# SwiGLU blocks behind the mixers all as seven-product quads, in a streaming-encoder trunk

## The chip, the core and the metric

The kernel runs on one core of a Trainium2 chip. The time is what the device measures from start to end of one execution, in microseconds (us); smaller is better. The engines are PE (matmul, with PEld for its weight loads), DVE (vector), ACT (scalar), POOL and SP, which here only issues loads. Each works through its own queue of instructions in a fixed order, and semaphores hold an instruction until what it needs is there.

## What is computed

Two layers of an encoder trunk, 512 frames of width 1024, inner width 2816, all in float32. The part that matters here is the end of the mixer and the second SwiGLU of a layer:

```python
def rmsnorm(x, g):
    return x * rsqrt(mean(x * x, -1) + EPS) * g

def swiglu(x, w_gu, w_down):
    g, u = split(x @ w_gu, 2, axis=-1)
    return (silu(g) * u) @ w_down

for i in range(DEPTH):                       # DEPTH = 2
    h = h + 0.5 * swiglu(rmsnorm(h, ffn1_norm[i]), ffn1_w_gu[i], ffn1_w_down[i])
    ...
    h = h + merged @ w_o[i]
    h = h + 0.5 * swiglu(rmsnorm(h, ffn2_norm[i]), ffn2_w_gu[i], ffn2_w_down[i])
    ...
```

## The kernel before

**Layout and precision.** Activations stand transposed, as eight tiles h[k] of 128 channels by 512 tokens. Each float32 operand is split into a rounded part (hi) and the rest (lo), and a product takes three matmuls, hi x hi, hi x lo, lo x hi (`mm3`, L266). Weights come in chunks of 1024 columns: SP loads a raw chunk into one of ten buffers (`st`, L52), ACT casts hi (`wh`, L71) and DVE subtracts for lo (`wl`, L72), into four pairs of buffers.

**Whole blocks and quads.** The inner width is 22 blocks of 128. A *whole* block takes 48 matmuls of 512 columns, gate and up. A *quad* (class `Sevens`) makes two blocks, both with gate and up, by seven products on halves (Strassen in Winograd's form, two halves of the tokens, of the inputs and of the block pair). Products 1, 2, 6, 3, 4 are *joint* steps (`joint`, L520): 8 matmuls of 512 columns (wide) and 8 of 256 (narrow). Products 5 and 7 are 24 matmuls of 256 columns (`product`, L540). Four raw quarters a11, a21, a22, a12 of the weights are combined by DVE (class `Quad`, L130), and the sums of the tokens stand in `Halved`: `own` (L464) makes what needs one row of h, `other` (L476) what needs the row four further on, each with casts on ACT and subtractions on DVE. Sums in PSUM: product 1 goes to b, ACT copies b into a (`seed`, L549) where product 2 is added, product 6 goes on in b, ACT copies b into d, where 5 and 3 are added, and 7 and 4 go on in b.

**PSUM** has eight banks. `paired` (L223) gives them out as two pairs for b, one pair for a and d, and two single banks `mp` for downs, output products and 1/rms.

**The mixer's end.** Eight output products of 24 matmuls (L1058), each into a single bank, are added to h[m] by DVE (L1060). `normed` (L357) follows behind each: x[k] = h[k] times the gain, split on ACT and DVE, the square on ACT, the sum of squares on DVE.

**The second SwiGLU** (`ffn`, from L588; its names begin with b0 in layer 0 and b1 in layer 1). Two blocks are whole, 20 are in quads 1 to 10. PE computes block 0 (L712), then two matmuls for the mean of the squares (`rms`, L342), and ACT and DVE make 1/rms while PE does quad 1's product 1; block 1 stands between quad 1's steps. A finished pair of values is multiplied by 1/rms, goes through Silu and is split (`finish`, L599). The downs (`down`, L637) of four blocks into one output row are 12 matmuls on a bank into which ACT has written 2h and which ACT writes back halved; `fill` (L651) puts them between the steps of the following quads (`next_quad`, L656).

What sets the order: a scheduler places instructions on each engine's queue from the program's order and its own estimates; `issue_after` holds a group behind a named instruction.

Of the kernel before, what the change touches and what calls it, by code (L numbers as in the profile page):

```python
# [129 lines left out]
class Quad:  # L130


    def __init__(self, W, quarters):
        self.W = W
        for q in ("a11", "a21", "a22", "a12"):
            setattr(self, q, W.raw(quarters[q]))

    def part(self, j):

        W = self.W  # L140
        tt = W.nc.vector.tensor_tensor
        if j == 1:
# [16 lines left out]
        return W.split(self.a11)  # L159


# [21 lines left out]
def trunk_kernel(ctx, tc, dims, x, p, positions, gains, rope_c, final_row, weights, out):  # L183
# [19 lines left out]
    class Banks:  # L203
# [18 lines left out]

        def paired(self):  # L223
            self.close()
            self.chain, self.seeded, self.single = self.pool("bp", 2), self.pool("ap", 1), self.pool("mp", 2)

# [12 lines left out]
    def PA(name):  # L239
        return two(banks.seeded, name)  # L240

    def halves(t):
# [15 lines left out]
    def split_to(hi, lo, src, scale=None):  # L258
        if scale is None:
            nc.scalar.copy(hi, src)  # L260
            return nc.vector.tensor_tensor(lo, src, hi.bitcast(F32), ALU.subtract)
        else:
            nc.scalar.activation(hi, src, AF.Copy, scale=scale)  # L263
            return nc.vector.scalar_tensor_tensor(lo, src, scale, hi.bitcast(F32), ALU.mult, ALU.subtract)
# [91 lines left out]

    def normed(nm, l, name, after=None, paired=True):  # L357

        xs, sq = [], Squares(name)
        for k in range(KD):  # L360
            xs.append(split(h[k], f"{name}x{k}", gain(nm, l, k), paired))
            sq.add(h[k])
            if after:
                after(k, xs)
        return xs, sq.parts()
# [81 lines left out]
    class Halved:  # L447
# [11 lines left out]
        def row(self, j, xs):  # L459

            self.own(j, xs)
            self.other(j, xs)

# [12 lines left out]
        def other(self, j, xs):  # L476

            H = S // 2
            left, right = slice(0, H), slice(H, S)
            k = j + KD // 2  # L480
            x, t, th, tl = self.half.pop(j)
            y, u = G(f"{self.name}y{j}"), G(f"{self.name}u{j}")
            nc.scalar.mul(y, h[k], gain(self.nm, self.l, k))
            nc.vector.tensor_tensor(t[:, right], y[:, right], x[:, right], ALU.subtract)
            nc.vector.tensor_tensor(u[:, left], t[:, right], x[:, left], ALU.add)
            nc.vector.tensor_tensor(u[:, right], y[:, left], u[:, left], ALU.subtract)
            split_to(th, tl, t)
            self.ys[7].append((th[:, right], tl[:, right]))
            for p_, at in ((2, left), (3, right)):
                self.ys[p_].append(self.both(xs[k], at))  # L490
            for p_, at in ((6, left), (4, right)):
                v = G(f"{self.name}u{j}_{p_}", F32R).rearrange("p (a t) -> p a t", t=H)
                split_to(v[:, 0, :], v[:, 1, :], u[:, at])
                self.ys[p_].append((v[:, 0, :], v))

    class Sevens:
# [7 lines left out]
        def __init__(self, w, l, name, ys, columns, done):  # L504
            self.w, self.l, self.name, self.ys, self.columns, self.done = w, l, name, ys, columns, done
            self.todo = {}
            self.narrow_first = ()

# [10 lines left out]

        def joint(self, ps, d, j):  # L520

            hi, lo = d["w"].part(j)
            at = [slice(i * P, (i + 1) * P) for i in range(8)]
            def wide(last):
                for k, (_, pair) in enumerate(self.ys[j]):
                    for w in range(2):
                        nc.tensor.matmul(ps[:, w, :].rearrange("p (a t) -> p a t", t=self.H), hi[:, at[2 * k + w]], pair,
                                         start=j == 1 and k == 0, stop=last and k == 3, skip_group_check=True)

            def narrow(last):  # L530
                for k, (vh, _) in enumerate(self.ys[j]):
                    for w in range(2):
                        nc.tensor.matmul(ps[:, w, :self.H], lo[:, at[2 * k + w]], vh, start=False, stop=last and k == 3,
                                         skip_group_check=True)

            parts = (narrow, wide) if j in self.narrow_first else (wide, narrow)
            for i, part in enumerate(parts):
                part(i == 1)

# [9 lines left out]
        def seed(self, n, what):  # L549
            d = self.todo[n]  # L550
            d[what] = PA(f"{self.name}{n}{what}")
            nc.scalar.copy(d[what].rearrange("p w t -> p (w t)"), d["b"].rearrange("p w t -> p (w t)"))

        def out(self, n, ps, f, c):
            t = self.tile(n, f"o{f}{c}")
            nc.scalar.copy(t, ps[:, :, self.H:])
            nc.vector.tensor_tensor(t, ps[:, :, :self.H], t, ALU.add)
            self.done(n, f, c, t, t)

        def step(self, n, j):  # L560
# [26 lines left out]

    def ffn(l, nm, name, first=False, beside=iter(()), early=2):  # L588

# [4 lines left out]
        ys = Halved(nm, l, name)  # L594
        n_whole = 4 if first else 2
        n0 = n_whole // 2
# [18 lines left out]
        if not first:  # L615
            sevens.narrow_first = (3, 4, 6)

        def early_rows(k, xs):

            if 0 <= k - KD // 2 < early:  # L620
                ys.row(k - KD // 2, xs)

        xs, acc = normed(nm, l, name, early_rows)

# [26 lines left out]
        def fill():  # L651
            if downs:
                m, f0 = downs.pop(0)
                down(m, f0, f0 + 4)

        def next_quad(n):  # L656

            for i, j in enumerate((1, 4, None, 2, 6, None, 5, 7, 3, None, None)):
                next(beside, None)
                if j is None:  # L660
                    if i < 9 or downs and downs[0][1] < f_last:
                        fill()
                    continue
                step(n if j == 4 else n + 1, j)
                if j == 6 and n % 2:
                    downs.extend((m, 2 * n - 2) for m in range(KD))

# [9 lines left out]
        if first:  # L677
# [22 lines left out]
            activate(3)  # L700
            downs.extend((m, 0) for m in range(KD))
            fill()
# [5 lines left out]
            for _ in range(2):  # L708
                fill()
        else:  # L710
            pss[0] = whole(0)
# [14 lines left out]
        fill()  # L726
        for n in range(n0, np_ - 1):
            next_quad(n)

        f0 = f_last  # L730
        left = [m for m in range(KD) if (m, f0) in downs]
        assert len(left) == len(downs)
# [25 lines left out]
    def mixer(l):  # L758
# [292 lines left out]
        for m in range(KD):  # L1051
# [4 lines left out]
            merged.append(split(t, f"{name}mg{m}"))  # L1056
        banks.paired()
        for m in range(KD):  # L1058
            ps = proj(W.col("w_o", l, m * P, D), merged, f"{name}wop{m}")
            nc.vector.tensor_tensor(h[m], ps, h[m], ALU.add)  # L1060
# [196 lines left out]
    for l in range(DEPTH):  # L1257
        ffn(l, "ffn1", f"a{l}", l == 0, rotary() if l == 0 else iter(()), 2 if l else 0)
        mixer(l)
        ffn(l, "ffn2", f"b{l}")  # L1260
        (ple_last if l == DEPTH - 1 else ple)(l)
# [48 lines left out]
```

## Time and profile before

| what | value |
|---|---|
| time, median of 3 runs | 2252.38 us (2252.13 to 2253.1) |
| the profiled execution's own time | 2252.33 us |
| its span, first to last instruction | 2250.3 us |
| PEld, busy | 1947.7 us (87%) |
| DVE, busy | 1743.5 us (77%) |
| ACT, busy | 1456.1 us (65%) |
| HBM | 98 GB/s over the span |

The profile shows each instruction with its start, its duration and what ended the idle time before it. Matmuls are pipelined: a matmul of 512 columns shows a duration of 0.39 us, but the next starts 0.23 us behind it, so PE is measured here from start to start. On ACT and DVE too a row starts some 0.1 us before the shown end of the row ahead, if it waits for nothing.

### The profile page before, as it was taken

How to read it: one execution, taken by the hardware profiler on the slowest of the kernel's cores; microseconds unless marked ns; L12 is line 12 of the kernel's file. 1: busy time of each engine (PE TensorE's matmuls, PEld its weight loads, DVE VectorE, ACT ScalarE, POOL GpSimd, SP SyncE). 2: the span in 40 equal slices, each digit the busy share in tenths (PEclk: the TensorE clock that was granted, in tenths of full speed). 3: DMA queues.
4: the chain of work that ended last, by engine and by line, in shares of the span. 5: the costliest groups of instructions: out<-in, count | busy, mean ns of one | idle time of the engine just before them, and what ended most of it. 6: DMA issues, size and time to landing. Idle time of an engine off the chain costs nothing.

```text
span 2250.3 us, 31142 instructions
## 1 busy us (share of the span) xinstructions
PE 2240.8 (100%) x12144; PEld 1947.7 (87%) x12144; DVE 1743.5 (77%) x2453; ACT 1456.1 (65%) x2246; POOL 37.4 (2%) x42
## 2 busy tenths in 40 slices
PE   9999999999999999999999999999999999999998
PEld 8888888888888888888888888888888888888887
DVE  8987768788866887776798777687889678777756
ACT  7666666576744666667676666764767357666664
POOL 0000000000200000000000000000001000000000
PEclk9999999999999999999999999999999999999999
DMA  5333332323132232334223233323222223333321
GB/s 215 99 113 104 103 122 75 112 76 104 47 104 84 94 103 97 107 107 141 75 94 104 96 106 108 113 88 102 92 76 75 94 75 103 104 104 103 108 99 38
DMA packets 63362, 223.04 MB, mean 99 GB/s; under 512 B 7280, under 2 KB 7280, under 8 KB 63216
## 3 DMA queue, kind: packets, MB, share of 16 engines
q1 hardware_dynamic: 62640, 220.28, 29.2%
q8 instruction: 95, 1.56, 0.3%
q10 hardware_dynamic: 576, 0.79, 0.1%
q14 instruction: 51, 0.42, 0.1%
HBM read 218.94 MB, written 2.10 MB: 98 GB/s over the span
## 4 chain that ended last, share of the span: by engine, by line
PE 97%; DVE 2%; ACT 1%; issue 0%; DVEq 0%
PE a0pd L268 2%; PE a1pd L268 2%; PE b0pd L268 2%; PE b1pd L268 2%; PE a0pd L269 2%; PE a0pd L270 2%; PE b1pd L269 2%; PE b0pd L269 2%; PE a1pd L269 2%; PE b1pd L270 2%; PE b0pd L270 2%; PE a1pd L270 2%; PE m0mop L268 1%; PE m1mop L269 1%; PE m0mop L269 1%; PE m1mop L270 1%
## 5 line engine op out<-in xcount | busy, mean ns | idle before, releaser
L72 DVE TENSOR_TENSOR wl<-st,wh 128x1024 fp32r<-128x1024 f32 (+1 forms) x508 | 614.7, 1212 | 227.5 <-ACT wh L71 224.1
L71 ACT CAST wh<-st 128x1024 fp32r<-128x1024 f32 (+1 forms) x507 | 527.9, 1044 | 306.6 <-PE m1Bp L269 13.9
L71 ACT CAST wh<-s 128x1024 fp32r<-128x1024 f32 x49 | 51.6, 1052 | 28.8 <-PE m1Cp L269 4.2
L72 DVE TENSOR_TENSOR wl<-s,wh 128x1024 fp32r<-128x1024 f32 x49 | 59.6, 1216 | 0.3 <-ACT wh L71 0.3
L152 DVE TENSOR_TENSOR st<-st,st 128x1024 f32<-128x1024 f32 x49 | 59.7, 1219 | 0.2
L154 DVE TENSOR_TENSOR s<-st,st 128x1024 f32<-128x1024 f32 x49 | 59.6, 1217 | 0.1
L149 DVE TENSOR_TENSOR st<-st,s 128x1024 f32<-128x1024 f32 x49 | 59.6, 1216 | 0.0
L157 DVE TENSOR_TENSOR st<-st,st 128x1024 f32<-128x1024 f32 x49 | 59.6, 1216 | 0.0
L644 ACT ACTIVATE h<-a0pd 128x512 f32<-128x512 f32 x40 | 23.7, 594 | 5.6 <-PE a0pd L270 5.3
L644 ACT ACTIVATE h<-b1pd 128x512 f32<-128x512 f32 x40 | 23.7, 592 | 4.9 <-PE b1pd L270 4.8
L644 ACT ACTIVATE h<-b0pd 128x512 f32<-128x512 f32 x40 | 23.7, 592 | 4.7 <-PE b0pd L270 4.6
L644 ACT ACTIVATE h<-a1pd 128x512 f32<-128x512 f32 x40 | 23.6, 591 | 4.5 <-PE a1pd L270 4.4
L640 ACT ACTIVATE a1pd<-h 128x512 f32<-128x512 f32 x40 | 24.0, 599 | 0.7
L640 ACT ACTIVATE b1pd<-h 128x512 f32<-128x512 f32 x40 | 23.9, 599 | 0.6
L640 ACT ACTIVATE b0pd<-h 128x512 f32<-128x512 f32 x40 | 23.9, 598 | 0.6
L640 ACT ACTIVATE a0pd<-h 128x512 f32<-128x512 f32 x40 | 23.9, 598 | 0.6
L107 POOL MEMSET wh<- 128x256 f32 x4 | 1.1, 314 | 1173.3 <-DVE wl L72 1173.3
L268 PE MATMUL a0p<-a0x,wh 128*128 128x512 f32 x44 | 17.1, 390 | 0.0
L269 PE MATMUL a0p<-a0x,wh 128*128 128x512 f32 x44 | 17.1, 390 | 0.0
L270 PE MATMUL a0p<-a0x,wl 128*128 128x512 f32 x44 | 17.1, 389 | 0.0
L263 ACT ACTIVATE b0x<-h,cols 128x512 fp32r<-128x512 f32 x8 | 5.8, 724 | 13.3 <-DVE h L1060 13.3
L263 ACT ACTIVATE b1x<-h,cols 128x512 fp32r<-128x512 f32 x8 | 5.8, 723 | 13.3 <-DVE h L1060 13.3
(6945 smaller groups left out, 7503.9 us busy)
## 6 DMA issues: line engine op xcount, KB each, us to landing
st<-in_weights SPq DMA_DIRECT2D x406, 512.0 KB, 3.3
h<-in_x SPq DMA_DIRECT2D x8, 256.0 KB, 5.4
st<-in_weights SPq DMA_DIRECT2D x7, 256.0 KB, 5.3
out<-e1d SPq DMA_DIRECT2D x4, 256.0 KB, 2.1
out<-fh SPq DMA_DIRECT2D x3, 256.0 KB, 2.2
e0pi<-in_p SPq DMA_DIRECT2D x2, 256.0 KB, 3.5
e1pi<-in_p SPq DMA_DIRECT2D x2, 256.0 KB, 3.8
fg<-in_final_row SPq DMA_DIRECT2D x2, 256.0 KB, 4.5
```

The lines of the kernel that those rows point to most:

```text
L71: self.nc.scalar.copy(hi[:, w], src[:, w])
L72: self.nc.vector.tensor_tensor(lo[:, w], src[:, w], hi[:, w].bitcast(F32), ALU.subtract)
L149: tt(self.a12, self.a12, self.s, ALU.subtract)
L152: tt(self.a11, self.a11, self.a21, ALU.subtract)
L154: tt(self.s, self.a22, self.a11, ALU.subtract)
L157: tt(self.a21, self.a21, self.a22, ALU.add)
L263: nc.scalar.activation(hi, src, AF.Copy, scale=scale)
L268: nc.tensor.matmul(ps, wh, vh, start=first, stop=False, skip_group_check=seeded)
L269: nc.tensor.matmul(ps, wh, vl, start=False, stop=False, skip_group_check=seeded)
L270: return nc.tensor.matmul(ps, wl, vh, start=False, stop=last, skip_group_check=seeded)
L640: nc.scalar.mul(ps, h[m], 2.0)
L644: nc.scalar.mul(h[m], ps, 0.5)
```

## The change

In the second SwiGLU of both layers (`quads=True`) blocks 0 and 1 become quad 0, and there are no whole blocks.

- The weights of quad 0 are loaded and combined while the mixer's output product runs (`early`): parts 1 and 2 are split in halves of 512 columns into activation buffers, the sums for the other five are made at once.
- The output products are done in the order 0, 4, 1, 5, 2, 6, 3, 7, two of them into one tile of two banks, in turn the pair of a and d and a third pair (`PX`). `normed` follows the same order, and behind each row come `own` or `other`, so the last row of token sums stands ahead of the cast of the squares and of 1/rms.
- PE then does quad 0's product 1, the wide half of quad 1's product 1, the two matmuls for 1/rms (into the third pair), quad 0's 2 and 6, the narrow half of quad 1's product 1, quad 0's 5, 7, 3 (d of quad 0 in the third pair). Then the third pair is given back as two single banks.
- Blocks 0 and 1 go down alone (6 matmuls for each output row), then 2 and 3; the rest in fours as before.

The core of the diff:

```diff
+    def early(self, split):
+        tt = self.W.nc.vector.tensor_tensor
+        self.ready[1] = split(self.a11)
+        self.ready[2] = split(self.a12)
+        tt(self.a11, self.a11, self.a21, ALU.subtract)
+        self.s = self.W.buffer("s")
+        tt(self.s, self.a22, self.a11, ALU.subtract)
+        tt(self.a12, self.a12, self.s, ALU.subtract)
+        tt(self.a21, self.a21, self.a22, ALU.add)
+        self.summed = True
...
-        def paired(self):
+        def paired(self, spare=False):
...
+            if spare:
+                whole, self.scope = self.scope, ExitStack()
+                self.spare = self.pool("xp", 1)
+                self.part, self.scope = self.scope, whole
+            else:
+                self.single = self.pool("mp", 2)
+        def spare_to_singles(self):
+            self.part.close()
+            self.single = self.pool("mp", 2)
...
+            j = k - KD // 2
+            if quads:
+                ends[:] = [ys.own(k, xs) if j < 0 else ys.other(j, xs), split_to.hi]
...
+                if n == 0 and j == 1 and quads:
+                    sevens.seed(1, "a")
+                else:
+                    step(n if j == 4 else n + 1, j)
+                if j == 6 and (n % 2 or quads and n == 0):
+                    downs.extend((m, max(2 * n - 2, 2 if quads and n else 0), 2 * n + 2) for m in range(KD))
...
+        elif quads:
+            sevens.where[0, "d"] = PX
+            last_row, last_act = ends
+            with tc.issue_after(proj.last.ins):
+                step(0, 1)
+            first, second = sevens.opened(1)
+            with tc.issue_after(sevens.last):
+                wide_ins = first()
+            r = rms(acc, D, name, ps=halves(PX(name + "ps"))[0])
+            with tc.issue_after(wide_ins):
+                step(0, 2)
+            step(0, 6)
+            with tc.issue_after(sevens.last):
+                narrow_ins = second()
+            with tc.issue_after(last_row), tc.issue_after(last_act), tc.issue_after(narrow_ins):
+                step(0, 5)
+                step(0, 7)
+                step(0, 3)
+            banks.spare_to_singles()
+            with tc.issue_after(last_row), tc.issue_after(last_act):
+                next_quad(0)
...
-        banks.paired()
-        for m in range(KD):
-            ps = proj(W.col("w_o", l, m * P, D), merged, f"{name}wop{m}")
+        banks.paired(True)
+        for i, m in enumerate(halfway):
+            if i % 2 == 0:
+                pss = halves((PX if i % 4 else PA)(f"{name}wop{i}"))
+            ps = proj(W.col("w_o", l, m * P, D), merged, None, pss[i % 2])
             nc.vector.tensor_tensor(h[m], ps, h[m], ALU.add)
```

**Where instructions stand now.** On PE, at the change from the seventh to the eighth output product, before (m0wop is the product's bank, m0mg the merged input, wh and wl the weights):

```order
L269 MATMUL m0wop6_6756<-m0mg7l_6551,wh169_6771 128x512
L270 MATMUL m0wop6_6756<-m0mg7h_6550,wl169_6772 128x512
L268 MATMUL m0wop7_6788<-m0mg0h_6335,wh169_6771 128x512 [waits DVE_49]
L269 MATMUL m0wop7_6788<-m0mg0l_6336,wh169_6771 128x512
L270 MATMUL m0wop7_6788<-m0mg0h_6335,wl169_6772 128x512
```

The same place of PE after the change:

```order
L312 MATMUL m0wop6_6753<-m0mg7l_6551,wh169_6768 128x512
L313 MATMUL m0wop6_6753<-m0mg7h_6550,wl169_6769 128x512
L311 MATMUL m0wop6_6753<-m0mg0h_6335,wh169_6768 128x512 [waits DVE_49]
L312 MATMUL m0wop6_6753<-m0mg0l_6336,wh169_6768 128x512
L313 MATMUL m0wop6_6753<-m0mg0h_6335,wl169_6769 128x512
```

Before, that wait was for the add of h5, two products back; now both halves are of one tile, and the wait is for the add of h3, from the half that has just ended.

On ACT, around 1/rms of layer 0 before (b0t3h and b0u3 are the last row of token sums, b0r, b0t and b0ms belong to 1/rms, b01a is quad 1's second sum):

```order
L350 ACT_TABLE_LOAD
L350 ACTIVATE b0r_6975<-b0ps_6972,eps_t_85 128x512
L483 ACTIVATE b0y3_7009<-h7_96,cols_78 128x512
L351 ACTIVATE b0t_6976<-b0r_6975 128x512
L352 ACTIVATE b0ms_6977<-b0ps_6972,eps_t_85 128x512
L260 CAST b0t3h_7007<-b0t3_7004 128x512
L552 COPY b01a_7062<-b01b_7041 128x1024
```

The same place of ACT now, with b0ah the cast of the squares, and b00a and b00d the sums of quad 0:

```order
L303 CAST b0u3_6_6966<-b0u3_6959 128x256
L303 CAST b0u3_4_6969<-b0u3_6959 128x256
L303 CAST b0ah_6972<-b0acc_6848 128x512
L71 CAST wh173_7080<-st130_6818 128x1024
L71 CAST wh174_7110<-st129_6816 128x1024
L393 ACT_TABLE_LOAD
L393 ACTIVATE b0r_7019<-b0ps_7016,eps_t_85 128x512
L604 COPY b00o00_7043<-b00a_6993 128x512
L394 ACTIVATE b0t_7020<-b0r_7019 128x512
L395 ACTIVATE b0ms_7021<-b0ps_7016,eps_t_85 128x512
L71 CAST wh175_7143<-st132_6822 128x1024
L600 COPY b00d_7070<-b00b_6976 128x1024
```

The last row's casts have moved ahead of 1/rms, and the copy into d stands behind all of it.

On ACT between quad 0's last step and quad 1's copy into d, now (b0pd0 are the banks of the downs of blocks 0 and 1, b00o10 and b0a1h belong to block 1, b01d is quad 1's d):

```order
L71 CAST wh180_7286<-st134_6997 128x1024
L706 ACTIVATE b0pd0_0_7261<-h0_89 128x512
L706 ACTIVATE b0pd0_1_7276<-h1_90 128x512
L659 ACTIVATE b00o01_7163<-b00o01_7163 128x256
L71 CAST wh181_7316<-st133_6995 128x1024
L303 CAST b0a0h_7169<-b0an0_7048 128x512
L604 COPY b00o10_7199<-b00b_6976 128x512
L71 CAST wh182_7350<-st136_7001 128x1024
L659 ACTIVATE b00o10_7199<-b00o10_7199 128x256
L303 CAST b0a1h_7205<-b0an1_7141 128x512
L604 COPY b01o00_7229<-b01a_7177 128x512
L710 ACTIVATE h0_89<-b0pd0_0_7261 128x512
```

Before, blocks 0 and 1 were whole and their downs began a quad later, with blocks 2 and 3; now the first downs stand right behind quad 0, and the write-back of h0 stands ahead of quad 1's copy into d.

More of the change, by code (lines that the diff above doesn't have):

```diff
@@ L240, in PA, with PX @@
         return two(banks.seeded, name)
+    def PX(name):
+        return two(banks.spare, name)
     def halves(t):
@@ L355, in rms, with normed @@
         return r
[L357 to L361, printed above, removed]
+    def normed(nm, l, name, after=None, paired=True, order=range(8)):
+        xs, sq = [None] * KD, Squares(name)
+        for k in order:
+            xs[k] = split(h[k], f"{name}x{k}", gain(nm, l, k), paired)
             sq.add(h[k])
@@ L532, in narrow @@
                     for w in range(2):
-                        nc.tensor.matmul(ps[:, w, :self.H], lo[:, at[2 * k + w]], vh, start=False, stop=last and k == 3,
-                                         skip_group_check=True)
+                        end = nc.tensor.matmul(ps[:, w, :self.H], lo[:, at[2 * k + w]], vh, start=False, stop=last and k == 3,
+                                               skip_group_check=True)
+                return end.ins
             parts = (narrow, wide) if j in self.narrow_first else (wide, narrow)
+            if apart:
+                return [lambda last=i == 1, part=part: part(last) for i, part in enumerate(parts)]
             for i, part in enumerate(parts):
-                part(i == 1)
+                self.last = part(i == 1)
         def product(self, ps, d, j):
@@ L616, in ffn, with pieces @@
             sevens.narrow_first = (3, 4, 6)
+        ends = []
         def early_rows(k, xs):
-            if 0 <= k - KD // 2 < early:
-                ys.row(k - KD // 2, xs)
-        xs, acc = normed(nm, l, name, early_rows)
+            j = k - KD // 2
+            if quads:
+                ends[:] = [ys.own(k, xs) if j < 0 else ys.other(j, xs), split_to.hi]
+            elif 0 <= j < early:
+                ys.row(j, xs)
+        if quads:
+            def pieces(src):
+                parts = [split(src[:, c:c + 512], f"{name}q{c}") for c in (0, 512)]
+                return Pieces([a for a, _ in parts]), Pieces([b for _, b in parts])
+            sevens.quad(0)["w"].early(pieces)
+        xs, acc = normed(nm, l, name, early_rows, order=halfway if quads else range(KD))
         pss, pds = {}, {}
@@ L652, in fill @@
             if downs:
-                m, f0 = downs.pop(0)
-                down(m, f0, f0 + 4)
+                m, f0, f1 = downs.pop(0)
+                down(m, f0, f1)
+                if f1 == 2 and downs:
+                    m, f0, f1 = downs.pop(0)
+                    down(m, f0, f1)
         def next_quad(n):
@@ L700, in ffn @@
             activate(3)
-            downs.extend((m, 0) for m in range(KD))
+            downs.extend((m, 0, 4) for m in range(KD))
             fill()
@@ L726, in ffn @@
         fill()
-        for n in range(n0, np_ - 1):
+        for n in range(1 if quads else n0, np_ - 1):
             next_quad(n)
         f0 = f_last
-        left = [m for m in range(KD) if (m, f0) in downs]
+        left = [m for m in range(KD) if (m, f0, f0 + 4) in downs]
         assert len(left) == len(downs)
```

46 lines of the change are left out of this document (31 added, 15 removed).

## The prediction

> **What bounds the kernel now.** I read the page's busy times first, then the chain that ended last, then what PE waits for.
>
> ```profile
> PE 2240.8 (100%) x12144; PEld 1947.7 (87%) x12144; DVE 1743.5 (77%) x2453; ACT 1456.1 (65%) x2246; POOL 37.4 (2%) x42
> ...
> PE 97%; DVE 2%; ACT 1%; issue 0%; DVEq 0%
> ```
> ```profile
> PE idle L376 <- DVE hpi L305: 1.0, 1, 1.0
> PE m0cop L270 <- DVE wl L72: 0.3, 1, 0.3
> PE m1cop L270 <- DVE wl L72: 0.3, 1, 0.3
> ```
>
> PE is busy for all of the 2250.3 us span except its start and end, it is 97% of the chain, and all its waits sum to 1.6 us. So every microsecond of matmul taken out is a microsecond won, and every wait that PE gets is one lost. The next question is how much cover PE has where the change acts, at the second mixer output and the start of the second SwiGLU (the stretches by engine: busy time of PE, weight load, DVE, ACT, POOL, then the granted clock and the DMA):
>
> ```profile
> 690.00:729.00 39.00, 39.00 (x174) 32.30 (x173) 27.53 (x42) 20.75 (x31) 0.00 (x0) 1.00 0.23 81
> 729.00:757.00 28.00, 28.00 (x136) 23.63 (x135) 25.68 (x38) 21.94 (x31) 0.00 (x0) 1.00 0.20 68
> ```
>
> While the output product runs (39 us) DVE and ACT have slack. In the 28 us behind it, DVE is busy 25.68 and ACT 21.94, and PE waits for neither only because its 48 matmuls of the first whole block need nothing but x and its weights. That cover is what the change takes away.
>
> **What PE gains.** Rows of PE behind it: a joint step (sums, then wide), and two products.
>
> ```profile
> 751.52 1.12 PE L533 MATMUL b01b<-b0u,wl 128*128 128x256 f32 x8
> 752.48 2.00 PE L527 MATMUL b01b<-b0u,wh 128*128 128x512 f32 x8
> 754.32 0.39 PE L268 MATMUL b0pu<-b0x,wh 128*128 128x512 f32 x1
> ...
> 759.76 0.28 PE L547 MATMUL b01d<-b0t0h,wh 128*128 128x256 f32 x1
> ...
> 765.51 1.12 PE L533 MATMUL b01d<-b0x,wl 128*128 128x256 f32 x8
> ```
>
> Eight matmuls of 256 columns take 752.48 - 751.52 = 0.96, eight of 512 take 1.84, so a joint step is 2.80. The 24 matmuls between 754.32 and 759.76 take 5.44, 0.2267 each. The two products take 5.75. Two whole blocks are 4 x 24 = 96 matmuls of 512 columns, 21.76 us; the quad that replaces them is 5 x 2.80 + 5.75 = 19.75. PE gains **2.0 us** for each of the two layers, and nothing else leaves PE: the downs have the same matmuls in other groups.
>
> **Term A, the pairs of the output product.** Now two outputs share one tile of two banks, and the first matmul of the second half waits for DVE's add to h from the first half (that add raises the count it waits for). What such a hand-over costs stands here, PE, then DVE, then ACT as a reader that follows DVE:
>
> ```profile
> 690.84 0.39 PE L270 MATMUL m0wop<-m0mg7h,wl 128*128 128x512 f32 x1
> 691.07 0.39 PE L268 MATMUL m0wop<-m0mg0h,wh 128*128 128x512 f32 x1
> ```
> ```profile
> 688.00 0.69 DVE L261 TENSOR_TENSOR m0mg7l<-m0g,m0mg7h 128x512 fp32r<-128x512 f32 x1 [0.76 <-ACT m0mg7h L260]
> 689.45 1.23 DVE L72 TENSOR_TENSOR wl<-st,wh 128x1024 fp32r<-128x1024 f32 x1 [0.76 <-ACT wh L71]
> 691.27 0.69 DVE L1060 TENSOR_TENSOR h<-m0wop,h 128x512 f32<-128x512 f32 x1 [0.59 <-PE m0wop L270]
> ```
> ```profile
> 692.00 0.73 ACT L263 ACTIVATE b0x<-h,cols 128x512 fp32r<-128x512 f32 x1 [2.58 <-DVE h L1060]
> ```
>
> Without a wait PE goes on at 691.07; the add starts 0.20 later, lasts 0.69, and a reader starts 0.04 behind it: 0.93 with an idle DVE. The order covers three of the four waits with seven, seven and six matmuls of the next pair (seven are 1.59); behind the last pair stands nothing. At the first pair the new rows stand ahead of the add: three 512-wide subtractions for quad 0, a 1024-wide sum and the split that was there (0.60 and 1.14 apart: back to back a row starts 0.09 before the shown end of the one ahead). They move the add from 691.27 to 692.7, PE goes on at 693.4 instead of 692.66: 0.75. At the last pair 18 matmuls follow the six pulled ahead (4.08 us), while DVE works off x6, the squares, two sums of the row and a split of 1.23: the add starts about 0.65 late, 0.93 + 0.65 = 1.6. A matmul behind a wait is itself slow:
>
> ```profile
> 503.07 0.40 PE L269 MATMUL m0cop<-m0yc0l,wh 128*128 128x512 f32 x1
> 503.74 0.50 PE L270 MATMUL m0cop<-m0yc0h,wl 128*128 128x512 f32 x1 [0.27 <-DVE wl L72]
> 504.08 0.40 PE L268 MATMUL m0cop<-m0yc1h,wh 128*128 128x512 f32 x1
> ```
>
> From 503.74 to 504.08 is 0.34 against 0.23, so 0.11 for each wait. A = 0.75 + 1.6 + 0.2 = **2.5**; bounds 0.93 (the one bare hand-over) and 3.7 (four).
>
> [...]
>
> **Term B, 1/rms and the seed of d.** Count from PE's first matmul of quad 0 as 0. Prices of ACT:
>
> ```profile
> 741.20 1.28 ACT L350 ACT_TABLE_LOAD   x1
> 742.49 0.69 ACT L350 ACTIVATE b0r<-b0ps,eps_t 128x512 f32<-128x512 f32 x1
> 743.08 0.71 ACT L483 ACTIVATE b0y<-h,cols 128x512 f32<-128x512 f32 x1
> 743.69 0.62 ACT L351 ACTIVATE b0t<-b0r 128x512 f32<-128x512 f32 x1
> 744.21 0.68 ACT L352 ACTIVATE b0ms<-b0ps,eps_t 128x512 f32<-128x512 f32 x1
> 744.78 0.62 ACT L260 CAST b0t3h<-b0t 128x512 fp32r<-128x512 f32 x1
> 745.29 1.02 ACT L552 COPY b01a<-b01b 128x1024 f32<-128x1024 f32 x1
> ```
> ```profile
> 753.11 0.58 ACT L556 COPY b01o<-b01a 128x512 f32<-128x512 f32 x1
> 754.58 1.05 ACT L71 CAST wh<-st 128x1024 fp32r<-128x1024 f32 x1 [0.89 <-PE b01b L527]
> 755.54 1.00 ACT L552 COPY b01d<-b01b 128x1024 f32<-128x1024 f32 x1
> 756.48 0.41 ACT L604 ACTIVATE b01o<-b01o 128x256 f32<-128x256 f32 x1
> ```
>
> Rows of ACT start some 0.1 before the shown end of the one ahead. h7 is added at 0.2 to 0.9; x7, its square and y run to 2.8; the seed of a (1.02) waits for PE's first joint step, to 4.0; then the last row's casts (0.62, 0.41, 0.41) and the cast of the squares end at 5.6, DVE's low half of them at 6.5. PE comes to the second sum matmul at about 6.3: 0.25 lost. ACT goes on: two weight casts (to 7.5), table (8.7), 1/rms (9.4), a copy (9.9), a square (10.4), the mean (11.0), a cast (11.9), and only then the seed of d, 11.9 to 12.9. PE has by then done 2.80 + 1.84 + 2.80 + 0.45 + 0.25 + 2.80 + 0.96 = 11.9 and needs it: 1.0, and 0.11. B = **1.4**. Bounds: 0 if the two casts are done before 0, 2.6 if both stand twice as long.
>
> **Term C, the second activation and quad 1's seed.** From 13.0 PE does j=5 and 7 (5.75), one matmul, j=3 and 4 (5.60), ends j=4 at 24.5, then the rest of quad 1's j=2 (2.55) and j=6 (2.80), and starts downs of block 0 at 29.9, six matmuls, to 31.2. It then needs block 1. DVE's prices here:
>
> ```profile
> 757.12 0.42 DVE L608 TENSOR_TENSOR b0an<-b01o 128x256 f32<-128x256 f32 x1
> ```
>
> After j=4, ACT has a weight cast, two writes of 2h into PSUM, a Silu, a cast and a0h before the copy of block 1's left half: that ends at 29.0. DVE's low half of a cast and a0l stand ahead of its add: 29.8 to 30.5, times 1/rms to 31.2, Silu to 31.6; the low half of the next cast (1.22) stands ahead of the last product, 32.2 to 32.65; a1h to 33.3. PE waits 2.1 (+0.11), and 0.3 for a1l. Then quad 1's d needs the tile that its a held: ACT copies that (33.8), writes back h0 after its last down matmul (34.8 to 35.4), seeds to 36.4. PE was ready at 35.1: 1.3 + 0.11. C = **4.0**. Without queues the path from j=4's end is 3.7 long and would end at 28.4, before PE: so the lower bound is 0; the upper is 5.7, one more cast on each of the two paths.
>
> **Term D, short downs and later.** Blocks 0 and 1 go down alone, and 2 and 3 after them: 16 downs of 6 matmuls (1.36 us) in the place of 8 of 12.
>
> ```profile
> L644 ACT ACTIVATE h<-a1pd 128x512 f32<-128x512 f32 x40 | 23.6, 591 | 4.5 <-PE a1pd L270 4.4
> L640 ACT ACTIVATE a1pd<-h 128x512 f32<-128x512 f32 x40 | 24.0, 599 | 0.7
> ```
>
> Each takes ACT 0.59 + 0.60; with two banks a pair of downs gives PE 2.72 of work, and one bank's round is 1.36 + 0.2 + 1.19 + 0.1 = 2.85. Where downs follow each other, and casts of 1.05 stand between, I take five waits of 0.3, and one seed of d late by 0.9 at quad 4, where the extra evacuations end. D = **2.4**, bounds 0 and 16 x 0.25 = 4. ACT's other additions (three casts 3.15, two seeds 2.0, four copies 2.3 per layer) lie beside PE but for the places in B and C. The loads cost nothing: SP holds as many as before, and quad 1's first weights stand some five casts ahead of their own; one that came late would move its cast, and PE, by as much.
>
> **Sum.** 2.5 + 1.4 + 4.0 + 2.4 - 2.0 = 8.3 for each layer; both layers run the same rows. 2252.33 (the profiled execution, 0.05 under the median) + 16.6 = **2269**.
>
> **Rivals.**
> - *The queues catch up.* If ACT's seed of d is ready 1.0 earlier and a1h 2.2 earlier, B, C and D go and only the pairs stay: 2.5 - 2.0 = 0.5 per layer, 2253.3, not slower. For: ACT idles 18 of the 39 us before 0, so casts could be done there; it turns on whether the two casts ahead of the table load run before 0. Against: they stand behind the cast of the squares, which needs h7. Chance 0.11. With the pairs free too, the gain stands alone: 2248.3, chance 0.02.
> - *Only C is hidden*, because earlier waits give DVE time: 4.3 per layer, 2261. For: PE's delays do shift its needs. Against: block 1's path starts at j=4's end and shifts with them. Chance 0.08.
> - *PE slows after a wait.* No wait of PE above is over 1.0 us, and the clock is 1.00 in both stretches. If the two products behind a wait of 2 us ran at half speed, 5.75 more per layer: 2280. Chance 0.04.
>
> [...]
>
> That the change does not do what it says I give nothing: its order shows the row ahead of 1/rms and the product in two parts.
>
> **Numbers.** The forecast has 0.75. The range takes the terms towards their bounds: A 1.5, B 0.7, C 1.5, D 0.6 leave 2.3 per layer, 2257; A 3.2, B 2.2, C 5.2, D 3.6 give 12.2, 2277. Left out are the catching up, the bare gain and the slow clock, 0.17. A measurement of this kernel tells 0.2% (4.5 us) from no change, so 2247.9 to 2256.9 is the same: 0.11; faster 0.02; slower 0.75 + 0.08 + 0.04 = 0.87.
>
> **What would show it.** PE idle in the waits of the changed trace: the last pair's second half behind DVE's add to h (1 to 1.8); d of quad 0 behind ACT (about 1); the first downs behind a1h (about 2); d of quad 1 behind ACT (1.3). If PE's idle time stays under 4 us in all, I am wrong, and the first place to look is ACT between 0 and 12. If PE's idle is as said and the time is not, the price of the quad is wrong.

## The result, and the profile after

| | us | runs | clock, mean over the run |
|---|---|---|---|
| before | 2252.41 (2252.08 to 2253.1) | 6 | 0.999 |
| changed | 2271.53 (2269.39 to 2271.74) | 6 | 0.997 to 0.999 |
| ratio | 1.0082, 95% interval 1.0069 to 1.0095 | | |

The changed kernel is slower by 19.1 us. The six times lie in two groups: 2269.39 and 2269.90, whose mean granted clock is 0.999 as before, and four from 2271.53 to 2271.74, at 0.997 or 0.998. The profiled execution (own time 2271.53, span 2269.5) is of the second group.

Busy time and the chain on the page of the changed kernel, the lines that answer to those of before:

```profile
PE 2246.3 (99%) x12208; PEld 1947.3 (86%) x12208; DVE 1766.3 (78%) x2483; ACT 1483.7 (65%) x2304; POOL 37.4 (2%) x42
...
PE 93%; DVE 4%; ACT 2%; issue 1%; ACTq 0%; DVEq 0%
```

PE is still 93% of the chain, but DVE and ACT now hold 6% of it, 3% before. What PE waits for (engine, tile and line, what ended the wait, us in total, times, longest):

```profile
PE b1pd L311 <- ACT b1a1h L303: 2.0, 1, 2.0
PE b0pd L311 <- ACT b0a1h L303: 2.0, 1, 2.0
...
PE m0wop L311 <- DVE h L1155: 2.0, 2, 1.4
PE b11d L595 <- ACT b11d L600: 1.2, 1, 1.2
...
PE b00d L595 <- ACT b00d L600: 1.0, 1, 1.0
PE b01d L595 <- ACT b01d L600: 0.8, 1, 0.8
PE b04d L595 <- ACT b04d L600: 0.7, 1, 0.7
```

Layer 1 has the same waits as layer 0, with names that begin with m1 and b1. Each new wait is one that the prediction named: the add to h in the output product, the seeds of d of quads 0, 1 and 4, and block 1's activation. Where the time arises is read from the same matmuls in both traces (first and last start of a group; before, then changed), at the second layer's mixer and in the last stage:

```profile
L268 PE MATMUL m1mop<-m1o00o,wh x8: 389/389/481, 1751.4 to 1794.6; 128*128 128x512 f32 x8
2182.71 0.39 PE L1121 MATMUL e1pp<-wh,e1p0h 128*128 128x512 f32 x1
```
```profile
L311 PE MATMUL m1mop<-m1o00o,wh x8: 389/389/481, 1762.0 to 1805.2; 128*128 128x512 f32 x8
2201.91 0.39 PE L1216 MATMUL e1pp<-wh,e1p0h 128*128 128x512 f32 x1
```

Up to the second mixer 10.6 us are lost, up to the last stage 19.2: layer 0 costs 10.6 and layer 1 8.6, though both issue the same instructions. The difference of 2.0 is that between the two groups of times. Here are the first products of quad 1's d in layer 0, then in layer 1 (PE's rows, the changed kernel):

```profile
768.42 0.58 PE L595 MATMUL b01d<-b0t0h,wh 128*128 128x256 f32 x1 [0.81 <-ACT b01d L600]
768.80 0.42 PE L595 MATMUL b01d<-b0t0l,wh 128*128 128x256 f32 x1
769.01 0.41 PE L595 MATMUL b01d<-b0t0h,wl 128*128 128x256 f32 x1
...
1893.71 0.38 PE L595 MATMUL b11d<-b1t0h,wh 128*128 128x256 f32 x1 [1.21 <-ACT b11d L600]
1893.93 0.28 PE L595 MATMUL b11d<-b1t0l,wh 128*128 128x256 f32 x1
1894.05 0.28 PE L595 MATMUL b11d<-b1t0h,wl 128*128 128x256 f32 x1
```

In layer 1 a matmul of 256 columns follows the one ahead by 0.12, in layer 0 by 0.21. The stretches (busy times, then granted clock) say why: half clock, and when it begins and ends.

```profile
766.50:767.00 0.50, 0.50 (x3) 0.33 (x2) 0.47 (x2) 0.15 (x1) 0.00 (x0) 0.53 0.61 246
773.00:773.50 0.50, 0.50 (x5) 0.50 (x4) 0.00 (x0) 0.00 (x0) 0.00 (x0) 0.65 0.00 0
1890.00:1895.00 5.00, 3.19 (x17) 2.26 (x18) 2.41 (x4) 3.89 (x8) 0.00 (x0) 1.00 0.34 110
```

A clock of 0.53 over half a microsecond, between 1.00 and 0.50, means that it fell at 766.53; 0.65 means that it rose at 773.35. It was low for 6.82 us, behind the wait of 2.03 for a1h, and not in layer 1.

### The profile page after: what moved, and what is told of

Its sections match the earlier page's. It is cut to its first block, busy times and chain, and to the rows that moved or that the text cites. A ratio compares the mean times of both kernels' runs of the same rounds, so it can differ in the third digit from the quotient of the medians.

```text
span 2269.5 us, 31385 instructions
## 1 busy us (share of the span) xinstructions
PE 2246.3 (99%) x12208; PEld 1947.3 (86%) x12208; DVE 1766.3 (78%) x2483; ACT 1483.7 (65%) x2304; POOL 37.4 (2%) x42
## 4 chain that ended last, share of the span: by engine, by line
PE 93%; DVE 4%; ACT 2%; issue 1%; ACTq 0%; DVEq 0%
PE a0pd L311 2%; PE a1pd L311 2%; PE a0pd L312 2%; PE a0pd L313 2%; PE a1pd L313 2%; PE a1pd L312 2%; PE b0pd L311 2%; PE b1pd L311 2%; PE b1pd L312 2%; PE b0pd L312 2%; PE b0pd L313 2%; PE b1pd L313 2%; DVE wl L72 1%; PE m0mop L313 1%; PE m1mop L313 1%; PE m1mop L311 1%
## 5 line engine op out<-in xcount | busy, mean ns | idle before, releaser
L710 ACT ACTIVATE h<-b1pd 128x512 f32<-128x512 f32 x48 | 28.3, 592 | 7.6 <-PE b1pd L313 7.5
L710 ACT ACTIVATE h<-b0pd 128x512 f32<-128x512 f32 x48 | 28.4, 593 | 7.5 <-PE b0pd L313 7.4
L706 ACT ACTIVATE b1pd<-h 128x512 f32<-128x512 f32 x48 | 28.7, 601 | 0.6
L706 ACT ACTIVATE b0pd<-h 128x512 f32<-128x512 f32 x48 | 28.7, 600 | 0.6
```

The costliest lines, as they stand in the source:

```text
L706: nc.scalar.mul(ps, h[m], 2.0)
L710: nc.scalar.mul(h[m], ps, 0.5)
```

## The experiments

The theory under test is the prediction's: PE gains 2.0 us per layer, and waits on DVE's and ACT's queues cost some 10 us per layer in return. Kernels are compared with the changed kernel's 2271.53; where no stretch of half clock is in them, the fair comparison is with its two runs without one, some 2269.6. The kernel before, run beside each group of experiments, took 2252.6 to 2252.8, so times of different groups may be set side by side.

**Products apart (x1).** Consecutive output products go to different bank pairs, so that a whole product lies between an add and the next use of its tile:

```diff
-            if i % 2 == 0:
-                pss = halves((PX if i % 4 else PA)(f"{name}wop{i}"))
-            ps = proj(..., None, pss[i % 2])
+            if i % 4 == 0:
+                pss = [halves(t(f"{name}wop{i}{k}")) for k, t in enumerate((PA, PX))]
+            ps = proj(..., None, pss[i % 2][i // 2 % 2])
```

> The output products alternate between the two bank pairs, so no product waits for the add to h of the product just ended. Theory (the waits at the pairs cost 0.77 + 0.10 + 1.56 + 0.11 = 2.54 us per layer, and PE's later waits move along with PE): 2271.5 - 5.1 = 2266.4, no wait for DVE's add to h in the output product, the waits for a1h (2.0), d of quad 0 (1.0) and d of quad 1 as they were. Rival (DVE and ACT are the bound there, so what is won at the pairs is waited for behind): d of quad 0 waits 2.5 longer and the time is 2271, within 1 us.

2266.57 (2266.49 to 2268.59, 5 runs), 4.96 less, at a clock of 0.998 in the median run, as in the changed kernel's second group. The waits for the add are gone, and what stands behind is unmoved:

```profile
PE b0pd L311 <- ACT b0a1h L303: 2.0, 1, 2.0
PE b00d L595 <- ACT b00d L600: 1.0, 1, 1.0
```

Term A stands by itself; the rival falls. The slowest of the five is the profiled one, with half clock in both layers, about which more below.

**Pairs alone (x6).** The kernel before, in which only the output products share tiles in pairs, in the order 0 to 7:

```diff
-        banks.paired()
+        banks.paired(True)
         for m in range(KD):
-            ps = proj(..., f"{name}wop{m}")
+            if m % 2 == 0:
+                pss = halves((PX if m % 4 else PA)(f"{name}wop{m}"))
+            ps = proj(..., None, pss[m % 2])
...
+        banks.spare_to_singles()
```

> The kernel before, with only its second mixer output's products put in pairs into two-bank tiles (outputs in order 0 to 7, whole first blocks as before). Theory (the hand-over inside a pair costs 0.93 only where DVE is busy with the quads' early sums and splits; seven matmuls of the next pair cover it elsewhere): at most 0.14 at each of three pairs, nothing at the last, 2252.4 + 0.8 = 2253.2. Rival (a pair costs its hand-over by itself): 0.93 + 0.11 at each of four pairs and both layers, 2260.7.

2253.98 (2253.43 to 2254.48, 11 runs) against 2252.81 beside it, ratio 1.0006 (0.9997 to 1.0014): nothing that can be told from no change, and PE waits for no add to h. A pair by itself is nearly free. At the last pair that is not because DVE is earlier. Here is its add to h in x6, then in the changed kernel, then what PE does meanwhile in x6:

```profile
725.18 0.68 DVE L1075 TENSOR_TENSOR h<-m0wop,h 128x512 f32<-128x512 f32 x1
```
```profile
725.27 0.68 DVE L1155 TENSOR_TENSOR h<-m0wop,h 128x512 f32<-128x512 f32 x1
```
```profile
724.82 0.39 PE L281 MATMUL b0p<-b0x,wh 128*128 128x512 f32 x1
```

In x6 PE fills the gap with five matmuls of block 0, from 724.82 to 725.95; the changed kernel has no whole block to take them from, and waits. So the larger half of the price, 1.56 of 2.54 per layer, is that of the missing cover at the last pair. The first pair's 0.77 is that of DVE's early sums and splits for quad 0, which stand ahead of the add: with most of them left out (x4, below) that wait is gone, and the last pair's stays at 1.1.

**Casts early (x3).** Quad 0's steps 5, 7, 3 and quad 1's steps are no longer held behind the last row of token sums:

```diff
-            with tc.issue_after(last_row), tc.issue_after(last_act), tc.issue_after(narrow_ins):
+            with tc.issue_after(narrow_ins):
                 step(0, 5)
...
-            with tc.issue_after(last_row), tc.issue_after(last_act):
+            if True:
                 next_quad(0)
```

> The steps j=5, 7, 3 of quad 0 and those of quad 1 are not held behind the last row of token sums: their weight casts may stand ahead of it. Theory (the holds keep ACT free for the last row; without them the seed of d comes later still): d of quad 0 waits 3.2 in place of 1.0, the last pair's wait is 1.3 in place of 1.56, others as they were, 0.9 per layer more... with both sides of the sum 2.2 - 0.3 = 1.9 per layer more: 2275. Rival (the two casts ahead of the table load are what makes d late, and would run in ACT's idle time during the output product): the 1.5 of term B go, 2268.5.

2277.31 (2277.09 to 2278.05, 4 runs): 5.8 more, 2.3 beyond the forecast, and half clock in both layers is part of that.

```profile
PE b00d L595 <- ACT b00d L600: 3.1, 1, 3.1
```

The seed of d comes later, not earlier, and ACT's rows of x3 show why:

```profile
736.44 1.05 ACT L71 CAST wh<-st 128x1024 fp32r<-128x1024 f32 x1 [0.90 <-PE b01b L571]
...
742.68 1.05 ACT L71 CAST wh<-st 128x1024 fp32r<-128x1024 f32 x1 [0.89 <-PE b00b L571]
```

Two casts did move into ACT's idle time ahead of the last row. But the two that now stand between the seed of a and that of d wait 0.90 and 0.89 for PE (to give a buffer of weights free, as I read it), and ACT's queue stands still behind them; the seed of quad 1's a, too, came ahead of that of d. The holds of the change were right for what it does.

**Downs in fours (x2).** Blocks 0 to 3 go down together, from quad 2 on:

```diff
-                if j == 6 and (n % 2 or quads and n == 0):
-                    downs.extend((m, max(2 * n - 2, 2 if quads and n else 0), 2 * n + 2) for m in range(KD))
+                if j == 6 and n % 2:
+                    downs.extend((m, 2 * n - 2, 2 * n + 2) for m in range(KD))
```

> Blocks 0 to 3 go down in one group of 12 matmuls per output, from quad 2 on, as in the kernel before; the short downs are gone. Theory (the waits of C and D are those of a DVE and an ACT that have more to do than PE in the first two quads): the waits for a1h (2.19 + 0.27 + 0.11) and of the short downs and quad 4's d (1.93) go, but nothing stands between quad 1's j=6 and its d any more; with the rows' durations in the queues, PE waits 1.3 for the bank pair of quad 2's b and 3.3 for quad 1's d in place of 1.37. Net 1.7 per layer less: 2268. Rival (the short downs are the cost by themselves): 2.57 + 1.93 = 4.5 per layer less: 2262.5.

2269.42 (2268.46 to 2269.75, 5 runs): 2.1 less, 3.5 were expected, and 9 by the rival. The waits of C and D have moved, as the theory said, to where 1.3 and 3.3 were forecast:

```profile
PE b01d L595 <- ACT b01d L600: 3.1, 1, 3.1
...
PE b02b L571 <- ACT wh L71: 1.1, 1, 1.1
```

With a gap of 3.1 in each layer the profile has half clock behind both, for 3.4 us each.

**The third pair kept (x7).** x1 and x2, and quad 1's d too goes into the third bank pair, which becomes the two single banks only behind quad 1:

```diff
-            sevens.where[0, "d"] = PX
+            sevens.where[0, "d"] = sevens.where[1, "d"] = PX
...
-            banks.spare_to_singles()
             with tc.issue_after(last_row), tc.issue_after(last_act):
                 next_quad(0)
+            banks.spare_to_singles()
```

> Products apart as in the first experiment, downs in fours as in the second, and quad 1's d goes into the third bank pair, which stays until quad 0 and 1 are done. Theory (queues): waits left per layer: d of quad 0 1.0, d of quad 1 1.3, a of quad 2 1.6, d of quad 2 0.9; none above 1.7, so the clock stays at 1.00 and all runs agree. 4.6 per layer less than 2269.6: 2260.4. Rival (the four-wise downs move their waits behind, as in the second experiment, and the bank pair changes nothing): 2263 or more, with quad 1's d at 3.

2260.38 (2260.35 to 2260.65, 5 runs), as forecast; ratio to the kernel before 1.0035 (1.0022 to 1.0047), the clock at 0.999 in all five.

```profile
PE b01d L595 <- ACT b01d L600: 1.1, 1, 1.1
```

Quad 1's d no longer waits for the bank that its a holds: its wait is 1.1, where x2 had 3.1, and so the rival falls. (x7 changes three things at once; what the bank pair alone is worth was not run.) This is the best complete form of the change that I ran, 11.2 us below it, 2 of them by the clock, and still some 8 above the kernel before.

**One split (x4).** To see whether the queues of DVE and ACT are the cause at all, their work is taken away and PE's left as it is: the kernel leaves out 12 of the 14 weight splits and all 8 weight sums of quads 0 and 1, and so does not compute the block.

```diff
+        if self.held:
+            return self.held
...
-            sevens.quad(0)["w"].early(pieces)
+            w0 = sevens.quad(0)["w"]
+            w0.held = pieces(w0.a11)
...
+            sevens.quad(1)["w"].held = w0.held
```

> Leaves out 12 of the 14 weight splits and all 8 weight sums of quads 0 and 1: all seven products of both quads take the split of quad 0's first quarter, so ACT and DVE have 12 casts, 12 low halves and 8 sums less per layer, and PE the same matmuls. Theory (the new waits are queues on DVE and ACT, the price of the quad on PE is right): the waits for a1h and quad 1's d (2.19 + 0.27 + 0.11 + 1.37) and the first pair's 0.77 go, the last pair's falls to 1.2; d of quad 0 (1.0), quad 4's d and the short downs stay: 4.9 per layer less, 2271.5 - 9.8 = 2261.7, and 2 less again if a slow stretch of the clock in layer 0 goes too. Rival (the quad costs PE more than 19.75, or the time is lost in reading weights or PSUM): PE's idle falls but the time stays within 3 us of 2271.5.

2260.33 (2259.68 to 2260.38, 5 runs), the clock at 0.999 in all: 11.2 less, or 9.3 less than the runs at that clock, where 9.8 were expected. The waits for a1h and quad 1's d are gone, those expected to stay stay, the last pair's among them:

```profile
PE m0wop L313 <- DVE h L1159: 1.1, 1, 1.1
```

The rival is refuted: PE has the same matmuls, and the time falls with its waits. Late loads are no rival either: in the changed kernel's trace no idle time of ACT or DVE from 738 to 800 us was ended by a load.

**The bare gain (x9).** x7 and x4 together (so it leaves out what x4 leaves out), with j=6 ahead of j=2 in both quads and the refinement of 1/rms behind the seed of d:

```diff
             with tc.issue_after(wide_ins):
-                step(0, 2)
-            step(0, 6)
+                step(0, 6)
+            refine()
+            step(0, 2)
```

> Leaves out 12 of the 14 weight splits and all 8 weight sums of quads 0 and 1, as the fourth experiment, and stands on the seventh (products apart, downs in fours, quad 1's d in the third bank pair); j=6 comes ahead of j=2 in quads 0 and 1, and the square and the refinement of 1/rms come behind the seed of d. Theory (PE's gain is 2.0 us per layer, and all of the loss was waiting): no wait of PE between the output product and quad 4 over 0.2, 2252.5 - 4.0 = 2248.5. Rival (a quad costs PE more than 5 x 2.80 + 5.75, by the many losses under 0.08 that the changed kernel's rows show, 0.6 per layer more than before): 2249.7; or more than that, if the quad's price is wrong: 2251 to 2253 with PE never idle.

2248.65 (2248.0 to 2249.86, 11 runs) against 2252.58 beside it: 3.9 less, ratio 0.9983 (0.9974 to 0.9992). PE has no wait left in these stages. So PE's gain is real and sized right, 2.0 per layer; but it came only with most of DVE's and ACT's work for quads 0 and 1 left out, and no complete form that I ran has it. The stretch from 757 to 790 in three kernels, before, x7 and x9 (busy PE, weight load, DVE, ACT):

```profile
757.00:790.00 33.00, 33.00 (x212) 30.03 (x212) 25.75 (x34) 19.86 (x29) 0.00 (x0) 1.00 0.32 103
```
```profile
757.00:790.00 33.00, 29.64 (x175) 25.34 (x174) 27.86 (x36) 20.95 (x33) 0.00 (x0) 1.00 0.35 116
```
```profile
757.00:790.00 33.00, 33.00 (x218) 30.38 (x218) 19.38 (x28) 17.45 (x28) 0.00 (x0) 1.00 0.20 64
```

Where quads follow each other without downs between, DVE is busy for 27.86 of 33 us, and PE is the one that waits. DVE is not full even there: what PE waits for is a row that stands behind others in a queue. I read the whole blocks so: they were not only costlier work, but work that asked little of DVE, and so the time in which DVE got ahead. That fits x6 and these three rows; no run puts a whole block back to test it.

**Sums on GpSimd (x8).** x7, and GpSimd makes quad 1's weight sums, with j=6 ahead of j=2 in quad 1:

```diff
-        tt = W.nc.vector.tensor_tensor
+        tt = (W.nc.gpsimd if self.pool else W.nc.vector).tensor_tensor
...
-            for i, j in enumerate((1, 4, None, 2, 6, None, 5, 7, 3, None, None)):
+            for i, j in enumerate((1, 4, None, 6, 2, None, 5, 7, 3, None, None) if quads and n == 0 else
+                                  (1, 4, None, 2, 6, None, 5, 7, 3, None, None)):
...
+            sevens.quad(1)["w"].pool = True
```

> As the one before, and GpSimd does the four weight sums of quad 1 in DVE's place, and quad 1's j=6 comes ahead of its j=2. Theory (DVE's queue is what is late in the first two quads): with 4 us for a sum on GpSimd, which no run here shows yet (its 128 x 384 rows took 1.25 to 3.3), the waits for quad 1's d and quad 2's a go; d of quad 0 (1.0) and of quad 2 (0.9) stay: 7.4 per layer less than 2269.6, 2254.7, beside 2252.4 of the kernel before. Rival (GpSimd's sums take longer than the 15 us between them and their use, or slow DVE's rows beside them): 2258 or more, with DVE's 1024-wide rows longer than 1.22 in that stretch.

2260.54 (2260.25 to 2260.68, 5 runs), no gain on x7, so forecast missed by 5.8. Half of the theory holds: the waits for quad 1's d and quad 2's a are gone. In their place PE waits in quad 0's first steps (1.2 for x, 0.8 for the seed of a), and the rival's second half says why. GpSimd's rows, then DVE's at the same time, then DVE's rows of x7 for the same work:

```profile
719.18 2.41 POOL L170 TENSOR_TENSOR st<-st,st 128x1024 f32<-128x1024 f32 x1 [81.61 <-DVE wl L72]
721.66 2.73 POOL L172 TENSOR_TENSOR s<-st,st 128x1024 f32<-128x1024 f32 x1
724.34 2.85 POOL L175 TENSOR_TENSOR st<-st,st 128x1024 f32<-128x1024 f32 x1
```
```profile
720.49 1.65 DVE L307 SCALAR_TENSOR_TENSOR b0x<-h,cols,b0x 128x512 fp32r<-128x512 f32 x1 [0.79 <-ACT b0x L306]
722.05 2.88 DVE L380 TENSOR_TENSOR b0acc<-b0acc,b0sq 128x512 f32<-128x512 f32 x1
724.86 2.61 DVE L527 TENSOR_TENSOR b0t<-b0y,b0x 128x256 f32<-128x256 f32 x1
```
```profile
720.40 0.75 DVE L307 SCALAR_TENSOR_TENSOR b0x<-h,cols,b0x 128x512 fp32r<-128x512 f32 x1 [0.79 <-ACT b0x L306]
721.07 0.68 DVE L380 TENSOR_TENSOR b0acc<-b0acc,b0sq 128x512 f32<-128x512 f32 x1
721.68 0.41 DVE L527 TENSOR_TENSOR b0t<-b0y,b0x 128x256 f32<-128x256 f32 x1
```

Three rows that take DVE 1.84 alone take 7.14 beside GpSimd's three sums; DVE itself does such a sum in 1.22 (x7), so 3.66 for the three. Moving these three sums from DVE to GpSimd cost DVE more than it saved.

**A longer wait (x5).** ACT copies block 1's activation five times ahead of its cast:

```diff
             if whole:
+                for k in range(5 if quads and i == 1 else 0):
+                    nc.scalar.copy(G(f"{name}pad{k}"), acts[i])
                 acts[i] = split(acts[i], f"{name}a{i}")
```

> ACT copies block 1's activation five times into spare buffers ahead of its cast: 5 x 0.52 = 2.6 us more before a1h, nothing else changes. The wait for a1h becomes 4.7 in place of 2.0, quad 1's d waits 0.9 less: 1.9 per layer more, so 2269.6 (the runs with the clock at 0.999) + 3.8 = 2273.4. On the clock: theory (the clock is set on a grid of 3.41 us, and halves for the next stretch when a stretch was idle for more than about half): a gap of 4.7 leaves at least 2.3 idle in one stretch wherever the grid lies, so the clock halves in both layers in every run, and the time is 2275 to 2278, with less spread than before. Rival (the halving in layer 0 had another cause than idle time): layer 1 stays at 1.00 as in the changed kernel's profile and the times still come in two groups, 2273.4 and 2275.5.

2276.23 (2275.65 to 2276.40, 4 runs), the clock at 0.996 in all four, half clock in both layers of the profile. The spread is 0.8 where the changed kernel's is 2.4. So a longer wait of PE is enough to halve the clock, in layer 1 too, and the rival falls. The wait is 4.6 here, so x5 does not tell how much idle time it takes.

**The changed kernel again (x10).** Nothing edited.

> The changed kernel once more, nothing edited. Theory (the clock is set on a grid of 3.41 us that lies anywhere against the program, so each layer's 2.0 us wait halves it or not by chance): the times fall into groups 2 us apart, 2269.5 with the clock at 0.999, 2271.5 and 2273.5 below it, and where the profile shows a slow stretch it lasts 3.41 or 6.83, in layer 0 or in layer 1. Rival (something in layer 0 alone halves it): never in layer 1, and never 2273.5.

2269.93, 2269.95 (clock 0.999), 2271.68, 2271.75, 2271.94 (0.997, 0.998): two groups again, 2 us apart. No run at 2273.5, and the profile has the slow stretch in layer 0 once more, so on this the rival did better. That layer 1 cannot halve is not so: x1 halves in both layers behind the same wait. The grid (3.413 us, worked out in the last section) may explain why it did not here, but that is argued, not shown: behind a slow stretch in layer 0 the waits of layer 1 lie 1125.35 us on (765.25 and 1890.60 in the changed kernel), which is 329.7 times 3.413, another place on the grid; if layer 0 stays at full clock, they lie 2 us less on, 329.1 times, nearly the same place, which stays harmless. Whether that rules out 2273.5, or eleven runs were too few to meet it, is open.

## Why the prediction was right or wrong

The forecast was 2269, range 2257 to 2277, slower; measured 2271.53. What PE loses by each term in layer 1 (start to start, less the matmul's own step):

| term | forecast | measured |
|---|---|---|
| A, pairs | 0.75 + 1.6 + 0.2 = 2.5 | 0.77 + 1.56 + 0.21 = 2.54 |
| B, 1/rms and d | 1.4 | 0.21 + 1.19 + 0.10 = 1.5 |
| C, a1h and quad 1's d | 4.0 | 2.19 + 1.37 + 0.48 = 4.04 |
| D, short downs and quad 4's d | 2.4 | 0.97 + 0.96 = 1.93 |
| gain of PE | 2.0 | 3.93 / 2 = 2.0 (x9) |

**A** was right in place and size: the second halves of the first and of the last pair. So was its reason for the last, that nothing stands behind it: x6, where block 0 does, has the same late add and no wait.

```profile
1818.40 0.50 PE L311 MATMUL m1wop<-m1mg0h,wh 128*128 128x512 f32 x1 [0.61 <-DVE h L1155]
...
1851.34 0.50 PE L311 MATMUL m1wop<-m1mg0h,wh 128*128 128x512 f32 x1 [1.40 <-DVE h L1155]
```

By the forecast's own term these waits are 2 x 2.5 = 5.0 for both layers. x1, in which PE goes on in the other bank pair while DVE adds, gave 4.96 back, and no wait for the add is left.

**B** was right: ACT's queue up to the seed runs as counted. PE's first matmul of quad 0 starts at 731.59, so the table stood forecast at 739.1 and the seed at 743.5 (ACT's rows, the changed kernel).

```profile
739.13 1.28 ACT L393 ACT_TABLE_LOAD   x1
...
743.52 1.03 ACT L600 COPY b00d<-b00b 128x1024 f32<-128x1024 f32 x1
```

**C** was right to the row: the low half of the next cast stands ahead of block 1's last product on DVE, and ACT waits 1.05 for it.

```profile
763.00 1.22 DVE L72 TENSOR_TENSOR wl<-st,wh 128x1024 fp32r<-128x1024 f32 x1
764.13 0.42 DVE L663 TENSOR_TENSOR b0an<-b00o 128x256 f32<-128x256 f32 x1
```
```profile
764.58 0.62 ACT L303 CAST b0a1h<-b0an 128x512 fp32r<-128x512 f32 x1 [1.05 <-DVE b0an L663]
```

**D** was 0.5 too high. Three waits of 0.15 to 0.25 came in the place of "five waits of 0.3"; quad 4's d, 0.85 and 0.11, was right. (One bound was wrong in itself: B's upper one, 2.6. The two casts fill 1.9, from 5.6 to 7.5, so standing twice as long they would give 3.3.)

**The sum** of the waits is 10.0 in place of 10.3, but layer 1 costs 8.6, not 10.0 - 2.0 = 8.0. The rest, 0.6, goes with losses that are each too small for the rows (under 0.08); their sum in the layer is 0.7 more than before. I had not counted these. That the sum came within 0.6 of the runs at full clock is therefore luck in part: per layer, D 0.5 too high and these losses left out nearly cancel.

**The clock** is where a step failed. The sum has no term for it, though its own wait of 2.1 for a1h is twice the longest in the trace of before (1.0), and that trace does not show what the clock does behind a wait of 2. The changed trace does: the clock fell to 0.50 behind a wait of 2.03, in the larger group of runs, and that cost 2.0 us. My rival *PE slows after a wait* had the effect and the place, the two products behind the 2 us wait, but both layers and 5.75 for each; in the changed kernel it is one layer, and 23 of the 48 matmuls start at half clock. Its chance of 0.04 was far too low. Of the 2.5 us between 2269 and 2271.53, 2.0 is this.

The other rivals fell. *The queues catch up* would need the seed of d a microsecond earlier; in x3, with the casts free to run ahead, two of them did, and it came 2.1 later. *Only C is hidden* asked that PE's delays give DVE time; C is as long in x1, with 2.5 us less delay ahead of it, as in the changed kernel. The price of the quad, named as the suspect if PE's idle was as said and the time not, is cleared by x9.

## What to carry to other kernels

A cheaper form of the work on the bounding engine gains only what the other engines can feed: look at every engine in the stage itself, with the new form in it, not over the span (DVE was busy 78% overall and 27.86 of 33 us here). Busy time alone does not decide it: in the kernel before, DVE was busy for 25.68 of the 28 us behind the output product, and PE waited for nothing, as it had a whole block to do that needs only x and its weights. What decides is what stands in the queues ahead of the row that PE needs next. The costly form may be the cover of its neighbours. Where a wait comes from a shared tile, try first whether another place for the tile removes it: with other places for the output products and for one d, and the downs regrouped, x7 took 11.2 us off, 2 of them by the clock, and left out no work. And if the bounding engine gets waits of 2 us, add to the price the clock that it may lose behind them (2.0 us here, for one stretch of 6.82 at half clock).

## What the runs showed of the hardware

**PE's clock on a grid.** Half clock came behind waits of 2.0 to 4.6 us (2.03 in the changed kernel and x1, 3.1 in x2 and x3, 4.6 in x5), and its starts and ends lie on a grid, a row of windows, stretches of time of equal length. x1 has it in both layers, behind one wait of 2.03 each and nothing else of over 1.2 near (stretches of half a microsecond in which the clock changes):

```profile
763.50:764.00 0.50, 0.50 (x2) 0.39 (x2) 0.50 (x2) 0.00 (x0) 0.00 (x0) 0.74 1.02 369
770.50:771.00 0.50, 0.50 (x6) 0.50 (x5) 0.00 (x0) 0.00 (x0) 0.00 (x0) 0.94 0.00 0
1886.50:1887.00 0.50, 0.50 (x4) 0.36 (x2) 0.47 (x2) 0.10 (x1) 0.00 (x0) 0.72 0.82 336
1893.50:1894.00 0.50, 0.50 (x6) 0.50 (x5) 0.00 (x0) 0.25 (x1) 0.00 (x0) 0.95 0.00 0
```

By the clock's mean it fell at 763.74 and 1886.72 and rose at 770.56 and 1893.55: 6.82 and 6.83 long, and in x2 both are 3.41 long. The two falls are 1122.98 apart in x1 and in x2, 1126.40 in x5 and 1129.81 in x3: these distances differ by 3.42 and 3.41, the length of the short stretches, and are 329, 330 and 331 times 3.4133 (1122.98 / 329), which is my estimate of a window. Where the first 3.41 us of a stretch held no wait of PE, it ended with them (x2 in both layers, x3 in layer 1); where they held 0.8 us or more of a wait, it lasted twice as long (the other seven stretches). How much idle time it takes is less clear. In x1 a wait of 2.03 in each layer was enough. In x4 and x7, whose longest waits are 1.1 and 1.5, the clock stayed at 0.999 in all ten runs. Whether a limit lies between these, and where, the runs do not settle. A wait of 2.03 in x3 and in layer 1 of the changed kernel left the clock at 1.00, so its place on the grid seems to count: in the changed kernel, 766.53 + 329 x 3.4133 = 1889.51 is the end of a window, and splits the wait from 1888.57 to 1890.60. But if windows end just where the clock changes, x3's hold 1.87 and 1.94 of the wait in one piece and stay harmless, while x10's holds 1.64 of it and halves the clock; a simple limit fits only if the clock changes 0.15 us or more behind the end of a window, which nothing here shows.

**DVE beside GpSimd.** During GpSimd's 128x1024 sums of two SBUF operands (2.41 to 2.85 us each), DVE's rows of two SBUF operands took 1.65 to 2.88 in the place of 0.41 to 0.75 (x8, above): each ends 0.3 to 0.6 behind the end of the GpSimd row that it met. A DVE row with one operand in PSUM that started during such a sum was not held (0.69). GpSimd's fourth sum of layer 0, and two DVE rows beside it, the first with its operand d in PSUM:

```profile
754.38 2.47 POOL L167 TENSOR_TENSOR st<-st,s 128x1024 f32<-128x1024 f32 x1 [27.18 <-issue]
```
```profile
755.04 0.69 DVE L605 TENSOR_TENSOR b00o<-b00d,b00o 128x512 f32<-128x512 f32 x1 [0.46 <-ACT b00o L604]
755.76 1.63 DVE L658 TENSOR_TENSOR b00o<-b00o,b0r 128x512 f32<-128x512 f32 x1
```

The first took its usual 0.69 while GpSimd ran; the second, started 1.09 before GpSimd's end, took 0.94 longer than its usual 0.69.
